# Hybrid decoder trunk on one core: the second mixer's weight rests, guards and gate products move from GpSimd to VectorE, and its convolution reads PSUM

## The chip, the cores and the metric

The kernel runs on one core of a Trainium2 chip. The metric is the device time of one execution in microseconds (us); lower is better. Engines are named as the profile names them: PE is TensorE (matmul), PEld its weight load, DVE VectorE, ACT ScalarE, POOL GpSimd, SP SyncE, which issues the DMAs.

## The reference, cut to what matters

The trunk has two layers. Each is a token mixer (layer 0: Mamba-2 SSD; layer 1: RG-LRU) and a gated convolutional MLP, each with an RMSNorm before and after it. The change is in the second mixer:

```python
LRU_WIDTH = 1280; LRU_HEADS = 10; LRU_CONV = 4; LRU_C = 8.0; SEQ = 512; D_MODEL = 1024

def causal_dwconv(x, w, b):
    k = w.shape[0]
    s = x.shape[1]
    xp = jnp.pad(x, ((0, 0), (k - 1, 0), (0, 0)))
    y = b
    for j in range(k):
        y = y + xp[:, j:j + s, :] * w[j]
    return y

def rglru_mixer(u, w_in, b_in, conv_w, conv_b, w_gx, b_gx, w_ga, b_ga, lam, w_out, b_out):
    proj = u @ w_in + b_in
    ybr = jax.nn.gelu(proj[..., :LRU_WIDTH])
    xbr = causal_dwconv(proj[..., LRU_WIDTH:], conv_w, conv_b)
    xh = xbr.reshape(bsz, s, LRU_HEADS, LRU_BLOCK)
    gx = jax.nn.sigmoid(einsum('bshi,hij->bshj', xh, w_gx) + b_gx)
    ga = jax.nn.sigmoid(einsum('bshi,hij->bshj', xh, w_ga) + b_ga)
    log_a = LRU_C * ga * jax.nn.log_sigmoid(lam)
    a_t = jnp.exp(log_a)
    mult = jnp.sqrt(-jnp.expm1(2.0 * log_a))
    b_t = mult * gx * xbr
    _, h = lax.associative_scan(_linear_combine, (a_t, b_t), axis=1)
    return (h * ybr) @ w_out + b_out
```

All inputs are float32. The convolution sees zeros ahead of the first token, and the input bias b_in is part of what it sees from the first token on.

## The kernel before, in words

Everything lies transposed: 128 channels on the partitions, the 512 tokens along the free dimension. Each float32 product is three fp32r matmuls. A weight tile is split by `Weight` (lines 199 to 214) into a high part (an ACT copy, line 209) and a low part, the rest (a subtraction, line 210, on DVE unless the argument `lo` names another engine). `Act` (line 234) splits an activation in the same way (lines 240 and 241). `up_mm` (lines 223 to 229) is one 128-channel tile of a projection: 24 matmuls of 512 tokens. A raw weight lies in one of four buffers `r` until its rest has been taken, so the next load of that buffer waits for the rest.

The second mixer is `lru` (line 556). It has three stages.

1. Ten channel tiles m of the recurrent branch. For each: the projection into a PSUM bank; an ACT copy to SBUF that adds the input bias (line 578), after which the bank is free; the convolution of four taps (`conv`, line 297: one ACT instruction for tap 3 and the bias, then three DVE instructions, line 300, for the other taps); the split of the result; six gate matmuls (lines 585 to 587); two sigmoids on ACT (lines 593 and 594); the product of one gate with the branch (line 597, DVE); a guard, max(gate, 0), on POOL (line 598); a Tanh on ACT (line 599). The projections have four PSUM banks, the gates four.
2. Once the last Tanh is done, ten exponentials (line 606, ACT, after a table load), five instructions each of lines 608 and 609 (DVE), 610 and 613 (ACT) and 615 (DVE) on 1024 columns, and ten scans (line 617, DVE).
3. Ten projections of the gating branch, which need the weights alone and are run by PE among the stages above; their GELUs (line 625) follow the last square root; the product of scan and GELU (line 628) is on POOL. Then `down` (line 254) multiplies by `w_out`: 24 matmuls (line 251) for each of ten tiles.

In the mixer the rests of the 16 projection tiles that `lru` loads itself and of its three gate weights are taken on POOL (`lo=G`). The constants (taps, biases, the rate lambda) are laid out once by `late_consts` (line 696) during the first mixer.

Program order on each engine is not written by hand: the Tile framework schedules the instructions by its own timing model, and each engine then runs its list in order, waiting on semaphores. So an instruction whose operand is late holds up all that stand behind it on its engine.

Of the kernel before, what the change touches and what calls it, by code (L numbers as in the profile page):

```python
# [10 lines left out]
AF = mybir.ActivationFunctionType  # L11
ALU = mybir.AluOpType

P = 128
# [7 lines left out]
LW = 1280  # L22
NL = LW // P
# [52 lines left out]
def tile_trunk(ctx: ExitStack, tc: tile.TileContext, x, norm_mix_pre, norm_mix_post, norm_ffn_pre, norm_ffn_post,  # L76
               ssd_w_in, ssd_conv_w, ssd_conv_b, ssd_dt_bias, ssd_a_log, ssd_d, ssd_norm, ssd_w_out,
               lru_w_in, lru_b_in, lru_conv_w, lru_conv_b, lru_w_gx, lru_b_gx, lru_w_ga, lru_b_ga,
               lru_lambda, lru_w_out, lru_b_out, ffn_w_up, ffn_conv_w, ffn_conv_b, ffn_w_down, out, layers=4):
# [3 lines left out]
    V, A, G, T = nc.vector, nc.scalar, nc.gpsimd, nc.tensor  # L83
# [7 lines left out]
    small_tiles = {n: cp.tile([r, w], F32, name=n) for n, r, w in (  # L91
        ("ident", P, P), ("nhalf", P, 4), ("ones", P, 1), ("mask", P, P), ("dch", P, NH // 2), ("hb32", NH, 4), ("hrow", 2, NH), ("dall", P, NH),
        ("cssd", P, 120), ("clru", P, 116), ("cffn0a", P, 128), ("cffn0b", P, 128), ("cffn1a", P, 128), ("cffn1b", P, 128),
        ("lam0", P, NL), ("lam1", P, NL), ("lam2", P, NL), ("lam3", P, NL), ("lam4", P, NL), ("pad", P, 16))}
    stats = cp.tile([P, 48, 4], F32, name="stats")

    def new_h(ph):
        return [cp.tile([P, 2, KD, 256], F32R, tag=n, name=f"{n}{ph}") for n in ("hh", "hl")]


    h = new_h(0)
    LO = Slots(cp, "w", 1024, range(NOP))
    LO.place()
    RAW, H4, S2 = Slots(cp, "r", 1024, range(NRAW)), Slots(cp, "v", 1024, range(N4)), Slots(cp, "t", 512, range(N2))
    PS = Slots(pp, "ps", 512, range(8))

    def row4():
        return (H4 if H4.ids else LO).get()

    def cols(h):  # L110
        return slice(h * 512, (h + 1) * 512)

    def load_gain(src):
        g = row4()
        dma(g.ap, src.rearrange("(o d) -> o d", o=1).to_broadcast([P, D]))
        return g
# [40 lines left out]
    def taps_of(a):  # L157
        return a.rearrange("j (m c) -> (j m) c", c=P)
# [61 lines left out]
    def up_w(w, c0, n=P, lo=None):  # L220
        return Weight([w[:, c0:c0 + n].rearrange("(k p) c -> p k c", p=P)], KD, KD * n, lo)
# [72 lines left out]
        return p  # L294


    def conv(dst, src, k, col):
        A.activation(dst, src, AF.Identity, bias=col(k), scale=col(k - 1))  # L298
        for s in range(1, k):
            V.scalar_tensor_tensor(out=dst[:, s:S], in0=src[:, 0:S - s], scalar=col(k - 1 - s), in1=dst[:, s:S],  # L300
                                   op0=ALU.mult, op1=ALU.add)
# [254 lines left out]
    def lru(h, prep, epilogue):  # L556
        w_in, w_out = lru_w_in[0], lru_w_out[0]
        M, X = PS.take(4), PS.take(4)
        clru, spl, spl2 = (consts[n] for n in ("clru", "spl", "spl2"))
        bt, th, at = ([row4() for _ in range(NL // 2)] for _ in range(3))  # L560
        wg = None
        first = ahead_of.pop(2)
        pts = [M.get() for m in range(4)]
        for tok in HALVES:
            for m in range(4):
                up_mm(pts[m], first[m], h, tok)
        for m in range(NL):
# [12 lines left out]
            conv(xb.ap, ub.ap, 4, lambda q: clru[:, 10 * q + m:10 * q + m + 1])  # L580
            xa = Act(xb.ap, LO)
            pg = [X.get(), X.get()]
            for i in range(2):
                b = 2 * (m % 4) + i
                T.matmul(pg[i].ap, wg.wh[:, b, :], xa.ah, start=True, stop=False)
                T.matmul(pg[i].ap, wg.wh[:, b, :], xa.al, start=False, stop=False)
                T.matmul(pg[i].ap, wg.wl[:, b, :], xa.ah, start=False, stop=True)
            if m % 4 == 3:
                wg.free()


            bm, thm, am = (s[m // 2].ap[:, cols(m % 2)] for s in (bt, th, at))
            A.activation(bm, pg[0].ap, AF.Sigmoid, bias=clru[:, 70 + m:71 + m])
            A.activation(am, pg[1].ap, AF.Sigmoid, bias=clru[:, 80 + m:81 + m])
            for s in pg:
                s.free()
            V.tensor_tensor(out=bm, in0=bm, in1=xb.ap, op=ALU.mult)
            G.tensor_scalar(out=am, in0=am, scalar1=0.0, scalar2=None, op0=ALU.max)
            last = A.activation(thm, am, AF.Tanh, scale=spl[:, m:m + 1])
            for s in (ub, xb, xa):  # L600
                s.free()
        ahead = [up_w(w_in, m * P, lo=G) for m in range(4)]
        with tc.issue_after(last.ins):
            for m in range(NL):
                am = at[m // 2].ap[:, cols(m % 2)]
                last = A.activation(am, am, AF.Exp, scale=spl2[:, m:m + 1])
        for j in range(NL // 2):
            V.scalar_tensor_tensor(out=bt[j].ap, in0=at[j].ap, scalar=1.0, in1=bt[j].ap, op0=ALU.add, op1=ALU.mult)
            V.scalar_tensor_tensor(out=at[j].ap, in0=at[j].ap, scalar=1.0, in1=th[j].ap, op0=ALU.add, op1=ALU.mult)
            A.activation(at[j].ap, at[j].ap, AF.Identity, bias=ones[:, 0:1])  # L610
        with tc.issue_after(last.ins):
            for j in range(NL // 2):
                last = A.activation(th[j].ap, th[j].ap, AF.Sqrt, scale=-1.0)
        for j in range(NL // 2):
            V.tensor_tensor(out=bt[j].ap, in0=bt[j].ap, in1=th[j].ap, op=ALU.mult)
            for i in range(2):
                V.tensor_tensor_scan(th[j].ap[:, cols(i)], at[j].ap[:, cols(i)], bt[j].ap[:, cols(i)], 0.0, op0=ALU.mult, op1=ALU.add)  # L617
        M.give(X)
        for m in range(NL):
            w, pt = ahead.pop(0) if ahead else up_w(w_in, m * P, lo=G), M.get()  # L620
            up_mm(pt, w, h, FULL)
            w.free()
            yb = S2.get()
            with tc.issue_after(last.ins):
                A.activation(yb.ap, pt.ap, AF.Gelu_apprx_tanh, bias=clru[:, 50 + m:51 + m])
            pt.free()
            hm = th[m // 2].ap[:, cols(m % 2)]
            G.tensor_tensor(out=hm, in0=hm, in1=yb.ap, op=ALU.mult)
            yb.free()
        for s in at + bt + [wg]:  # L630
            s.free()
        PS.give(M)
        bo = load_gain(lru_b_out[0])

        def biased(t, acc):
            mb = row4()
            for i in range(2):
                V.tensor_tensor(out=mb.ap[:, cols(i)], in0=acc[i].ap, in1=bo.ap[:, cols(i)], op=ALU.add)
                acc[i].free()
            epilogue(t, [mb])  # L640
            if t == NT - 1:
                bo.free()

        down(w_out, NL, lambda k: th[k // 2].ap[:, cols(k % 2)], lambda k: th[k // 2].free() if k % 2 else None, prep, biased, GT)
# [49 lines left out]
    consts = {}  # L694

    def late_consts(banks):
        clru = const_cols("clru", [taps_of(lru_conv_w[0]), rows_of(lru_conv_b[0]), rows_of(lru_b_in[0]), rows_of(lru_b_gx[0]),
                                   rows_of(lru_b_ga[0]), rows_of(lru_lambda[0]), rows_of(ssd_norm[0])], banks)
        consts["clru"] = clru

        lam = [small_tiles[f"lam{i}"] for i in range(5)]
        V.tensor_scalar(out=lam[0], in0=clru[:, 90:100], scalar1=-1.0, scalar2=None, op0=ALU.mult)
        spl = softplus(*lam[1:], lam[0])
        V.tensor_scalar(out=lam[0], in0=spl, scalar1=-8.0, scalar2=None, op0=ALU.mult)
        V.tensor_scalar(out=spl, in0=spl, scalar1=-4.0, scalar2=None, op0=ALU.mult)
# [24 lines left out]
    for ph in range(layers):  # L730
# [31 lines left out]
        h = nh  # L762
# [30 lines left out]
```

## Time and profile before

| what | value |
|---|---|
| median of 3 runs | 1713.21 us (1713.0 to 1713.45) |
| profiled execution, its own time | 1712.34 us |
| span of the profiled execution | 1710.6 us, 19926 instructions |
| PE busy | 1640.6 us (96%) |
| DVE busy | 920.0 us (54%) |
| ACT busy | 713.3 us (42%) |
| POOL busy | 291.9 us (17%) |
| granted PE clock over the span | 0.984 of full speed |

The span runs from the first to the last instruction; 1.7 us of the execution's own time lie around it. Busy shares are means over stages that have different limits, so the second mixer has to be read by itself: its first matmul starts at about 951 us and its output product is done at about 1153 us. The granted clock is the share of full TensorE speed that a stretch of the trace shows.

### The profile page before, as it was taken

To read this page: it belongs to the slowest core of one execution; us is meant where nothing else is said; L and a number is where in the kernel's file an instruction comes from. 1 tells how busy PE (TensorE), PEld (TensorE's weight loads), DVE (VectorE), ACT (ScalarE), POOL (GpSimd) and SP (SyncE) were. 2 spreads that over 40 slices of the span, in tenths; PEclk is the share of its full clock that TensorE was granted. 3 is DMA by queue.
4 is the path that set the end of the run, shared out by engine and by line. 5 is a ranking of instruction groups with operands and counts; after the bars stand their busy time and mean duration, and the time that the engine had idled before them with its cause. 6 is when DMAs were issued, how large, how long until landed. Compare 5 with 4: busy or idle time off the path is not lost.

```text
span 1710.6 us, 19926 instructions
## 1 busy us (share of the span) xinstructions
PE 1640.6 (96%) x7905; PEld 1361.9 (80%) x7905; DVE 920.0 (54%) x1122; ACT 713.3 (42%) x1072; POOL 291.9 (17%) x238
## 2 busy tenths in 40 slices
PE   7979999998999999999999999697999999999998
PEld 6858888787888888888888977586888888888886
DVE  6878886646544444443343575946644444443432
ACT  5385655435333333333332576534433333333331
POOL 1012121205111111110001466513111111110000
PEclk9989999999999999999999999898999999999999
DMA  7443432234332233332333123333422333223321
GB/s 202 114 117 101 119 94 83 87 101 135 110 88 85 87 86 87 86 96 92 109 111 111 32 82 103 109 113 87 124 85 80 95 86 87 86 75 103 115 78 50
DMA packets 235701, 166.25 MB, mean 97 GB/s; under 512 B 6604, under 2 KB 218808, under 8 KB 235608
## 3 DMA queue, kind: packets, MB, share of 16 engines
q1 hardware_dynamic: 235608, 164.98, 33.0%
q8 instruction: 62, 1.02, 0.2%
q14 instruction: 31, 0.25, 0.0%
HBM read 162.80 MB, written 2.16 MB: 96 GB/s over the span
## 4 chain that ended last, share of the span: by engine, by line
PE 84%; DVE 6%; ACT 3%; DMA 2%; POOL 2%; issue 2%; SPq 0%; DVEq 0%; POOLq 0%; ACTq 0%
PE ps L251 23%; PE ps L228 17%; PE ps L227 17%; PE ps L229 17%; PE ps L553 5%; DVE t L300 1%; PE ps L430 1%; DVE w L617 1%; DVE w L210 1%; ACT w L209 1%; PE ps L432 1%; PE ps L179 1%; DVE w L241 1%; PE ps L444 1%; DMA r<-in_ffn_w_up_dram 1%
## 5 line engine op out<-in xcount | busy, mean ns | idle before, releaser
L228 PE MATMUL ps<-hl,w 128*128 128x512 f32 (+2 forms) x1632 | 615.7, 378 | 5.8 <-DVE hl L183 5.8
L210 DVE TENSOR_TENSOR w<-r,w 128x1024 fp32r<-128x1024 f32 (+1 forms) x263 | 327.8, 1252 | 542.6 <-ACT w L209 338.5
L227 PE MATMUL ps<-hh,w 128*128 128x512 f32 (+2 forms) x1632 | 614.3, 378 | 5.2 <-ACT hh L182 2.2
L229 PE MATMUL ps<-hh,w 128*128 128x512 f32 (+2 forms) x1632 | 613.7, 377 | 0.0
L209 ACT ACTIVATE w<-r 128x1024 fp32r<-128x1024 f32 (+1 forms) x282 | 294.2, 1051 | 395.6 <-PE ps L228 137.4
L251 PE MATMUL ps<-w,w 128*128 128x512 f32 x1776 | 407.0, 391 | 13.0 <-DVE w L241 13.0
L251 PEld LDWEIGHTS ps<-w,w 128*128 128x128 f32 x1776 | 334.9, 189 | 82.9 <-DVE w L241 13.4
L228 PEld LDWEIGHTS ps<-hl,w 128*128 128x128 f32 (+1 forms) x1632 | 310.0, 190 | 61.6 <-DVE hl L183 6.7
L227 PEld LDWEIGHTS ps<-hh,w 128*128 128x128 f32 (+1 forms) x1632 | 309.5, 190 | 62.2 <-ACT hh L182 3.3
L229 PEld LDWEIGHTS ps<-hh,w 128*128 128x128 f32 (+1 forms) x1632 | 309.8, 190 | 53.8
L681 POOL TENSOR_TENSOR w<-t,t 128x512 f32<-128x512 f32 x48 | 61.6, 1284 | 461.7 <-DVE t L300 443.6
L300 DVE SCALAR_TENSOR_TENSOR t<-ps,cffn0a,t 128x511 f32<-128x511 f32 (+1 forms) x128 | 95.5, 746 | 18.7 <-ACT t L298 16.5
L300 DVE SCALAR_TENSOR_TENSOR t<-ps,cffn1a,t 128x511 f32<-128x511 f32 (+1 forms) x128 | 95.3, 746 | 15.9 <-ACT t L298 13.8
L553 PE MATMUL ps<-w,w 128*128 128x512 f32 x384 | 90.0, 392 | 3.5 <-DVE w L241 1.2
L162 POOL TENSOR_SCALAR stats<-stats 128x1 f32<-128x1 f32 x32 | 14.6, 457 | 442.8 <-ACT v L190 369.6
L298 ACT ACTIVATE t<-ps,cffn0b 128x512 f32<-128x512 f32 x64 | 49.3, 770 | 92.4 <-PE ps L229 92.4
L553 PEld LDWEIGHTS ps<-w,w 128*128 128x128 f32 x384 | 71.4, 188 | 19.9 <-DVE w L241 2.3
L298 ACT ACTIVATE t<-ps,cffn1b 128x512 f32<-128x512 f32 x64 | 49.3, 771 | 89.1 <-PE ps L229 89.1
L676 ACT ACTIVATE t<-t 128x512 f32<-128x512 f32 x64 | 40.5, 632 | 93.8 <-DVE t L300 93.8
L240 ACT ACTIVATE w<-w 128x512 fp32r<-128x512 f32 (+1 forms) x62 | 40.0, 648 | 53.6 <-PE ps L251 36.8
L210 POOL TENSOR_TENSOR w<-r,w 128x1024 fp32r<-128x1024 f32 (+1 forms) x19 | 49.4, 2609 | 32.2 <-ACT w L209 28.0
L300 DVE SCALAR_TENSOR_TENSOR t<-ps,cssd,t 128x509 f32<-128x509 f32 (+2 forms) x72 | 51.9, 736 | 3.6 <-ACT t L298 3.2
(174 smaller groups left out, 1068.1 us busy)
## 6 DMA issues: line engine op xcount, KB each, us to landing
r<-in_ffn_w_up_dram SPq DMA_DIRECT2D x128, 512.0 KB, 4.0
r<-in_ffn_w_down_dram SPq DMA_DIRECT2D x64, 512.0 KB, 3.6
r<-in_ssd_w_in_dram SPq DMA_DIRECT2D x40, 512.0 KB, 3.9
r<-in_lru_w_in_dram SPq DMA_DIRECT2D x20, 512.0 KB, 3.7
w<-cs_d SPq DMA_DIRECT2D x16, 512.0 KB, 5.2
r<-in_ssd_w_out_dram SPq DMA_DIRECT2D x16, 512.0 KB, 3.8
r<-in_lru_w_out_dram SPq DMA_DIRECT2D x10, 512.0 KB
xr<-in_x_dram SPq DMA_DIRECT2D x8, 256.0 KB, 4.3
```

Source lines behind the costliest of these rows:

```text
L209: A.activation(self.hi.ap[:, 0:n], r, AF.Copy)
L210: (lo or V).tensor_tensor(out=self.lo.ap[:, 0:n], in0=r, in1=self.hi.f[:, 0:n], op=ALU.subtract)
L227: T.matmul(o, w.wh[:, k, :], hh[:, :, k, :], start=(k == 0), stop=False)
L228: T.matmul(o, w.wh[:, k, :], hl[:, :, k, :], start=False, stop=False)
L229: T.matmul(o, w.wl[:, k, :], hh[:, :, k, :], start=False, stop=(k == KD - 1))
L240: A.activation(self.ah, ap, AF.Copy)
L251: T.matmul(acc[h].ap, x_[:, tk], w_[:, cols(h)], start=(first and i == 0), stop=(last and i == 2))
L298: A.activation(dst, src, AF.Identity, bias=col(k), scale=col(k - 1))
L300: V.scalar_tensor_tensor(out=dst[:, s:S], in0=src[:, 0:S - s], scalar=col(k - 1 - s), in1=dst[:, s:S], op0=ALU.mult, op1=ALU.add)
L553: T.matmul(acc.ap, a[:, tk], b[:, u, :], start=(j == 0 and u == 0 and i == 0), stop=(j == 7 and u == 1 and i == 2))
L676: A.activation(ga.ap, ga.ap, AF.Gelu_apprx_tanh)
L681: G.tensor_tensor(out=p[-1].ap[:, cols(m % 2)], in0=ga.ap, in1=va.ap, op=ALU.mult)
```

## The change

What it does, all in or for `lru`:

- the rests of the weights (line 210) that `lru` loads, 16 projection tiles and three gate weights, are taken on DVE; the guard (line 598) and the product with the GELU (line 628) are DVE instructions too;
- the ACT copy with the input bias (line 578) is gone. The convolution reads the projection in PSUM. The input bias times the sum of the taps is added to the convolution's own bias; the first three columns, which see fewer taps, are corrected by a DVE addition of 128x3 elements for each tile;
- `late_consts` works out that bias and the three corrections in a new constant `lcor` (11 DVE instructions of 128x10); the buffer takes the place of an unused one (`pad`).

```diff
@@ conv
-    def conv(dst, src, k, col):
-        A.activation(dst, src, AF.Identity, bias=col(k), scale=col(k - 1))
+    def conv(dst, src, k, col, bias=None):
+        A.activation(dst, src, AF.Identity, bias=col(k) if bias is None else bias, scale=col(k - 1))
         for s in range(1, k):
             V.scalar_tensor_tensor(out=dst[:, s:S], in0=src[:, 0:S - s], scalar=col(k - 1 - s), in1=dst[:, s:S],
                                    op0=ALU.mult, op1=ALU.add)
@@ lru
-                wg = Weight([w_[0, m:m + n].rearrange("h i o -> i h o") for w_ in (lru_w_gx, lru_w_ga)], n, n * 256, G)
+                wg = Weight([w_[0, m:m + n].rearrange("h i o -> i h o") for w_ in (lru_w_gx, lru_w_ga)], n, n * 256)
...
-                w, pt = up_w(w_in, LW + m * P, lo=G), M.get()
+                w, pt = up_w(w_in, LW + m * P), M.get()
                 up_mm(pt, w, h, FULL)
             w.free()
-            ub, xb = S2.get(), S2.get()
-            A.activation(ub.ap, pt.ap, AF.Identity, bias=clru[:, 60 + m:61 + m])
+
+            xb = S2.get()
+            conv(xb.ap, pt.ap, 4, lambda q: clru[:, 10 * q + m:10 * q + m + 1], lcor[:, m, 3:4])
             pt.free()
-            conv(xb.ap, ub.ap, 4, lambda q: clru[:, 10 * q + m:10 * q + m + 1])
+            V.tensor_tensor(out=xb.ap[:, 0:3], in0=xb.ap[:, 0:3], in1=lcor[:, m, 0:3], op=ALU.add)
             xa = Act(xb.ap, LO)
...
             V.tensor_tensor(out=bm, in0=bm, in1=xb.ap, op=ALU.mult)
-            G.tensor_scalar(out=am, in0=am, scalar1=0.0, scalar2=None, op0=ALU.max)
+            V.tensor_scalar(out=am, in0=am, scalar1=0.0, scalar2=None, op0=ALU.max)
             last = A.activation(thm, am, AF.Tanh, scale=spl[:, m:m + 1])
...
-        ahead = [up_w(w_in, m * P, lo=G) for m in range(4)]
+        ahead = [up_w(w_in, m * P) for m in range(4)]
...
-            w, pt = ahead.pop(0) if ahead else up_w(w_in, m * P, lo=G), M.get()
+            w, pt = ahead.pop(0) if ahead else up_w(w_in, m * P), M.get()
...
-            G.tensor_tensor(out=hm, in0=hm, in1=yb.ap, op=ALU.mult)
+            V.tensor_tensor(out=hm, in0=hm, in1=yb.ap, op=ALU.mult)
@@ late_consts
+        lcor = small_tiles["lcor"].rearrange("p (m j) -> p m j", j=4)
+        b, part = clru[:, 60:70], lam[2]
+        for q in range(4):
+            V.tensor_tensor(out=part if q else lam[3], in0=clru[:, 10 * q:10 * q + 10], in1=b, op=ALU.mult)
+            if q:
+                V.tensor_tensor(out=lam[3], in0=lam[3], in1=part, op=ALU.add)
+            if q < 3:
+                V.tensor_scalar(out=lcor[:, :, 2 - q], in0=lam[3], scalar1=-1.0, scalar2=None, op0=ALU.mult)
+        V.tensor_tensor(out=lcor[:, :, 3], in0=lam[3], in1=clru[:, 40:50], op=ALU.add)
+        consts["lcor"] = lcor
```

In the changed kernel the lines of `lru` from the product on stand one higher: 598 is the product, 599 the guard, 609 to 618 the second stage, 629 the product with the GELU; 581 is the correction. The scheduler writes the order anew. Three places of it, first on POOL, from the last guards of the first stage on. Before:

```order
L210 TENSOR_TENSOR w_1132_7789<-r_1130_7786,w_1131_7788 128x1024
L210 TENSOR_TENSOR w_1138_7801<-r_1136_7798,w_1137_7800 128x1024
L598 TENSOR_SCALAR w_1038_7145<-w_1038_7145 128x512
L210 TENSOR_TENSOR w_1135_7795<-r_1133_7792,w_1134_7794 128x1024
L598 TENSOR_SCALAR w_1039_7146<-w_1039_7146 128x512 x2
L210 TENSOR_TENSOR w_1154_7998<-r_1152_7995,w_1153_7997 128x1024
```

The guards of the last three tiles (w_1038, w_1039) stand behind weight rests. All 39 such rows leave POOL: between the norms of the layer's start and those of its end nothing is left on it. The second place is DVE at the end of the first stage and the start of the second. Before:

```order
L597 TENSOR_TENSOR v_1028_7135<-v_1028_7135,t_1102_7643 128x512
L597 TENSOR_TENSOR w_1029_7136<-w_1029_7136,t_1114_7704 128x512
L597 TENSOR_TENSOR w_1029_7136<-w_1029_7136,t_1123_7758 128x512
L608 SCALAR_TENSOR_TENSOR v_1025_7132<-w_1035_7142,v_1025_7132 128x1024
L608 SCALAR_TENSOR_TENSOR v_1026_7133<-w_1036_7143,v_1026_7133 128x1024
```

Now:

```order
L210 TENSOR_TENSOR w_1125_7796<-r_1123_7793,w_1124_7795 128x1024
L598 TENSOR_TENSOR w_1029_7147<-w_1029_7147,t_1105_7706 128x512
L241 TENSOR_TENSOR w_1114_7765<-t_1113_7759,w_1114_7765 128x512
L599 TENSOR_SCALAR w_1039_7157<-w_1039_7157 128x512
L210 TENSOR_TENSOR w_1149_8033<-r_1147_8030,w_1148_8032 128x1024
L598 TENSOR_TENSOR w_1029_7147<-w_1029_7147,t_1113_7759 128x512
L599 TENSOR_SCALAR w_1039_7157<-w_1039_7157 128x512
L210 TENSOR_TENSOR w_1144_7999<-r_1142_7996,w_1143_7998 128x1024
L609 SCALAR_TENSOR_TENSOR v_1025_7143<-w_1035_7153,v_1025_7143 128x1024
L210 TENSOR_TENSOR w_1154_8067<-r_1152_8064,w_1153_8066 128x1024
```

The last guard (L599) stands right behind the last product (L598), and rests (L210) stand between the steps. The third place is DVE from the last scans to the split of the first tile for the output product (L241, w_1179). Now:

```order
L616 TENSOR_TENSOR w_1029_7147<-w_1029_7147,w_1034_7152 128x1024
L629 TENSOR_TENSOR w_1030_7148<-w_1030_7148,t_1130_7875 128x512
L629 TENSOR_TENSOR w_1030_7148<-w_1030_7148,t_1132_7903 128x512
L618 SCALAR_TENSOR_TENSOR w_1032_7150<-w_1037_7155,v_1027_7145 128x512 x2
L618 SCALAR_TENSOR_TENSOR w_1033_7151<-w_1038_7156,v_1028_7146 128x512 x2
L210 TENSOR_TENSOR w_1182_8212<-r_1180_8209,w_1181_8211 128x1024
L629 TENSOR_TENSOR w_1031_7149<-w_1031_7149,t_1134_7931 128x512
L629 TENSOR_TENSOR w_1031_7149<-w_1031_7149,t_1136_7959 128x512
L618 SCALAR_TENSOR_TENSOR w_1034_7152<-w_1039_7157,w_1029_7147 128x512 x2
L241 TENSOR_TENSOR w_1179_8182<-w_1030_7148,w_1179_8182 128x512
```

Four products with the GELU (L629) and one rest now stand among the scans (listed as L618 SCALAR_TENSOR_TENSOR), ahead of that split; before, two rests of `w_out` stood there and no product.

## Rows read from the trace of the kernel before

**Rows 1.** PE's waits, 950 to 1110 us: who waited for whom, us in total, times, longest.

```profile
PE ps L251 <- DVE w L241: 13.0, 1, 13.0
PE ps L586 <- DVE w L241: 3.5, 3, 1.4
PE ps L585 <- ACT v L593: 2.3, 2, 1.4
```

**Rows 2.** Stretches of the second mixer: us, busy us (xcount) by engine, clock, DMA.

```profile
1060.00:1077.00 17.00, 17.00 (x76) 13.86 (x74) 17.00 (x12) 15.18 (x16) 6.44 (x2) 1.00 0.31 91
1077.00:1104.00 27.00, 12.39 (x54) 9.87 (x54) 27.00 (x17) 12.48 (x19) 18.49 (x9) 0.84 0.27 87
1104.00:1111.00 7.00, 7.00 (x20) 5.49 (x21) 6.17 (x8) 3.23 (x4) 2.88 (x1) 0.63 0.69 206
```

**Rows 3.** PE timeline: start us, us, engine line op out<-in xcount [idle before <-releaser].

```profile
977.28 0.40 PE L227 MATMUL ps<-hh,w 128*128 128x512 f32 x1
...
1103.81 8.49 PE L251 MATMUL ps<-w,w 128*128 128x512 f32 x25 [12.98 <-DVE w L241]
```

**Rows 4.** ACT timeline around the last sigmoid and the exponentials' table load.

```profile
1039.86 0.70 ACT L594 ACTIVATE w<-ps,clru 128x512 f32<-128x512 f32 x1
1044.17 1.06 ACT L209 ACTIVATE w<-r 128x1024 fp32r<-128x1024 f32 x1 [3.62 <-DMA r<-in_lru_w_in_dram]
...
1051.89 0.71 ACT L599 ACTIVATE w<-w,lam 128x512 f32<-128x512 f32 x1
1052.62 1.28 ACT L606 ACT_TABLE_LOAD   x1
```

**Rows 5.** POOL timeline: the last guards, and a rest in the second stage.

```profile
1046.22 2.94 POOL L598 TENSOR_SCALAR w<-w 128x512 f32<-128x512 f32 x2
...
1065.63 3.25 POOL L210 TENSOR_TENSOR w<-r,w 128x1024 fp32r<-128x1024 f32 x1 [1.24 <-ACT w L209]
```

**Rows 6.** DVE timeline from the second stage's start to the output product.

```profile
1055.29 4.57 DVE L608 SCALAR_TENSOR_TENSOR v<-w,v 128x1024 f32<-128x1024 f32 x2 [12.76 <-ACT w L606]
...
1066.53 3.43 DVE L609 SCALAR_TENSOR_TENSOR w<-w,w 128x1024 f32<-128x1024 f32 x1
1069.88 1.21 DVE L608 SCALAR_TENSOR_TENSOR w<-w,w 128x1024 f32<-128x1024 f32 x1
1071.02 1.21 DVE L609 SCALAR_TENSOR_TENSOR w<-w,w 128x1024 f32<-128x1024 f32 x1
...
1075.56 2.33 DVE L617 TENSOR_TENSOR_SCAN w<-w,v 128x512 f32<-128x512 f32 x2
1077.81 1.19 DVE L210 TENSOR_TENSOR w<-r,w 128x1024 fp32r<-128x1024 f32 x1
...
1095.52 4.36 DVE L617 TENSOR_TENSOR_SCAN w<-w,w 128x512 f32<-128x512 f32 x2
```

**Rows 7.** DVE's waits, 966 to 1104 us.

```profile
DVE t L300 <- ACT t L298: 14.0, 4, 6.3
...
DVE v L597 <- ACT v L593: 2.9, 2, 2.8
...
DVE w L241 <- ACT w L240: 2.8, 3, 1.3
DVE w L597 <- ACT w L593: 2.6, 2, 2.3
```

**Rows 8.** The convolution's line by tile: xcount: ns min/median/max, first and last start us.

```profile
L300 DVE SCALAR_TENSOR_TENSOR t<-ps,cffn1a,t x128: 735/748/753, 1199.9 to 1531.3; 128x511 f32<-128x511 f32 x64, 128x510 f32<-128x510 f32 x64
...
L300 DVE SCALAR_TENSOR_TENSOR t<-t,clru,t x30: 731/748/2892, 973.0 to 1033.7; 128x511 f32<-128x511 f32 x10, 128x510 f32<-128x510 f32 x10, 128x509 f32<-128x509 f32 x10
```

**Rows 9.** Prices by group, whole program: busy us, mean ns of one | idle before.

```profile
L241 DVE TENSOR_TENSOR w<-w,w 128x512 fp32r<-128x512 f32 x58 | 39.4, 684 | 6.2 <-ACT w L240 6.2
...
L284 DVE TENSOR_SCALAR t<-t 32x512 f32<-32x512 f32 x1 | 0.4, 407 | 0.0
L284 DVE TENSOR_SCALAR lam<-lam 128x10 f32<-128x10 f32 x1 | 0.2, 166 | 0.0
```

More of the change, by code (lines that the diff above doesn't have):

```diff
@@ L93, in tile_trunk @@
         ("cssd", P, 120), ("clru", P, 116), ("cffn0a", P, 128), ("cffn0b", P, 128), ("cffn1a", P, 128), ("cffn1b", P, 128),
-        ("lam0", P, NL), ("lam1", P, NL), ("lam2", P, NL), ("lam3", P, NL), ("lam4", P, NL), ("pad", P, 16))}
+        ("lam0", P, NL), ("lam1", P, NL), ("lam2", P, NL), ("lam3", P, NL), ("lam4", P, NL), ("lcor", P, 4 * NL))}
     stats = cp.tile([P, 48, 4], F32, name="stats")
@@ L558, in lru @@
         M, X = PS.take(4), PS.take(4)
-        clru, spl, spl2 = (consts[n] for n in ("clru", "spl", "spl2"))
+        clru, spl, spl2, lcor = (consts[n] for n in ("clru", "spl", "spl2", "lcor"))
         bt, th, at = ([row4() for _ in range(NL // 2)] for _ in range(3))
@@ L597, in lru @@
             V.tensor_tensor(out=bm, in0=bm, in1=xb.ap, op=ALU.mult)
-            G.tensor_scalar(out=am, in0=am, scalar1=0.0, scalar2=None, op0=ALU.max)
+            V.tensor_scalar(out=am, in0=am, scalar1=0.0, scalar2=None, op0=ALU.max)
             last = A.activation(thm, am, AF.Tanh, scale=spl[:, m:m + 1])
-            for s in (ub, xb, xa):
+            for s in (xb, xa):
                 s.free()
-        ahead = [up_w(w_in, m * P, lo=G) for m in range(4)]
+        ahead = [up_w(w_in, m * P) for m in range(4)]
         with tc.issue_after(last.ins):
```

## The prediction, as it stood before the changed kernel was timed

> **What bounds the kernel now.** I read PE's waits first, since PE is busy for 96% of the span and only its waits can be won. In the second mixer PE waits 13.0 us once, for the split that feeds the output product, and 3.5 and 2.3 us in the gates [rows 1]. That one wait is the largest in the stage. The stretches show who is late: from 1060 to 1077 us PE and DVE are both busy all the time, from 1077 to 1104 DVE is busy 27.0 of 27.0 us and PE 12.4 [rows 2]. [...] So the output product, which starts at 1103.81 us [rows 3], hangs on a chain of DVE work, and the reader should follow that chain backwards.
>
> It has two legs. The first goes from the end of the last sigmoid, 1039.86 + 0.70 = 1040.56 us, to the table load of the exponentials at 1052.62 us: 12.1 us [rows 4]. Between them there is nothing but a guard and a Tanh of 0.71 us, yet the last two guards start at 1046.22 us on POOL, behind weight rests in its queue, and the last Tanh at 1051.89 us [rows 4, 5]. DVE is idle for 12.76 us meanwhile [rows 6]. The second leg is DVE from 1055.29 us to 1103.81 us, 48.5 us [rows 3, 6]. In it instructions of one shape take two durations: line 609 takes 1.21 us at 1071.02 and 3.43 us at 1066.53, when POOL runs a rest from 1065.63 for 3.25 us; two scans take 2.33 us at 1075.56 and 4.36 us at 1095.52 [rows 5, 6]. The convolution shows the same, a median of 748 ns and a maximum of 2892 [rows 8]. DVE loses that time beside POOL, and all of this POOL work leaves.
>
> **First leg.** The guard becomes a DVE instruction of 512 columns with a scalar. No such row exists; bounds are 0.41 us, the same kind on 32 partitions, and 0.68 us, a two-input instruction of 512 columns [rows 9]. I take 0.41, the same kind. In the new order an ACT split of 1.06 us stands between the last sigmoid and the last Tanh [rows 4]; the guard lies beside it. So 1.06 + 0.71 = 1.8 us in place of 12.1: **-10.3 us**. The Tanh no longer waits for POOL's queue; what it can wait for instead is the load ahead of that ACT split (below).
>
> **Second leg.** From the first instruction of the new line 609 to the split for the output product the new order has 15 instructions of 1024 columns, ten scans, five weight rests, four products with the GELU and the split. Issue to issue a 1024-column instruction takes 1071.02 - 1069.88 = 1.14 us and a scan (1077.81 - 1075.56) / 2 = 1.13 us when POOL is quiet; a rest takes 1.19 us [rows 6], a 512-column instruction with two inputs 0.68 [rows 9]. That is 17.1 + 11.3 + 6.0 + 5 x 0.68 = 37.8 us in place of 48.5: **-10.7 us**, although rests and products are added. The later six products lie beside PE's 24 matmuls for each output tile, 24 x 17.0 / 76 = 5.4 us [rows 2], and cost nothing; without that cover they are 6 x 0.68 = 4.1 us.
>
> **Will the first stage end later?** DVE gains 30 taps read from PSUM at 0.75 (the same as now, see below), ten corrections at 0.17, nine guards at 0.41, 13 full rests at 1.19 and a half one at 0.68 before the last product, beside ten splits and ten products at 0.68 [rows 6, 8, 9]: 22.5 + 1.7 + 3.7 + 15.5 + 0.7 + 13.6 = 57.7 us. It starts at 973.0 [rows 8], so DVE could be done at 1030.7. Its waits of today, 14.0 + 2.9 + 2.8 + 2.6 less the 6.3 before the start, are 16.0 us [rows 7]. With all of them it ends at 1046.7, 6 us late; rows overlap by some 6% (1.21 against 1.14), which gives back 3. The ACT copy of about 0.7 us for each tile goes, and the rests free the raw buffers sooner. I take no change of the last sigmoid; bounds are -3 and +6.
>
> **Convolution from PSUM.** The row of the last MLP reads PSUM with the same instruction: 748 ns median, against 748 from SBUF [rows 8]. So the 30 taps cost nothing more. [...] A bank is now held until the third tap has run; four banks serve the projections, so this bites only if DVE is about four tiles late.
>
> **Clock.** If the wait shrinks, the 7 us at 0.63 become full speed: 7.0 x 0.37 = **-2.6 us** [rows 2]. Bound: 0, if a wait that is left brings the low clock back.
>
> **What is new.** Rests on DVE wait for loads, and what stands behind them on DVE waits too. Today such a wait sits on ACT: 3.62 us once for the load of a projection [rows 4]. I take **+2 us**, between none and 3.6. The first gate rest, amid the norms of the layer's start, is 1.19 us more on DVE, but POOL, which works out the norms' factors, loses it: 0, bounds -1.2 and +1.2. The 11 constant instructions are 11 x 0.17 = 1.9 us of DVE in the first mixer [rows 9], beside PE's matmuls; I take 0, with 1.9 either way, since the scheduler also reorders a few instructions there and in the second MLP.
>
> **Sum.** -10.3 - 10.7 - 2.6 + 2 = -21.6 us. The output product would start near 1103.8 - 21.0 + 2 = 1084.8. Can PE be there? From 977.28 us it has six projections, ten gate sets, ten more projections and the four matmuls ahead of the split: 16 x 24 + 60 + 4 = 448, at 17.0 / 76 = 0.224 us [rows 2, 3], so 1077.6 at the earliest. DVE stays the later of the two, with a wait of some 7 us left of the 13.0. The profiled execution took 1712.34 us; less 21.6 it is 1690.7. The median of the runs is 0.9 us above it, so I forecast **1691.6 us**. A measurement of this kernel tells about 0.2%, 3.4 us, from no change.
>
> **Rivals.**
> 1. *PE becomes the bound.* The gates also come sooner and PE never waits: the product starts at 1077.6, so 26.2 + 2.6 = 28.8 us are won, 1684.4 us. For it: DVE's 57.7 us of work leave room before 1040. Against it: the second leg's 37.8 us are in series with table load and exponentials. It is the low end of the range.
> 2. *DVE's queue becomes the bound in the first stage.* The order stays interleaved, but 6 us of late end remain (less 3 of overlap) and three rests, with what is behind them, wait 3.62 us for their loads: +3 + 10.9 on top of -23.6 gives -9.7, 1703.5 us; 1697 to 1709 by how many wait. For it: three engines hand each tile to and fro, and today's list holds 16.0 us of such waits. Against it: the rests free raw buffers sooner, so loads start sooner.
> 3. *No tile overlaps the next, and it is slower.* Then each tile goes alone through three ACT steps of the convolution, split and Tanh (2.1), three taps (2.25), correction (0.17), split (0.68), six matmuls (1.34), two sigmoids (1.40), product and guard (1.09) and a rest (1.19): 10.2 us. Ten from 973.0 end at 1075.0 in place of 1040.6, +34.4 - 23.6 = +10.8, 1724.0 us. The place is DVE's list in the first stage. It decides above (1040.6 - 973.0 + 23.6) / 10 = 9.1 us for each tile; today it is 6.8. Against it: the order has up to three tiles' taps interleaved.
> 4. *The gain is used up*: a first stage some 20 to 27 us later, at about 9.1 us for each tile, 1713.
>
> **How the numbers follow.** The forecast, 1686 to 1697, has 0.62: its legs are plain sums of undisturbed rows. Rival 1 beyond it, below 1686: 0.06. Rival 2: 0.19. Rival 4: 0.06. Rival 3: 0.07. Faster by over 0.2%: 0.62 + 0.06 + 0.19 = 0.87; same 0.06; slower 0.07. The range from 1685 to 1704 takes the forecast, the edge of rival 1 and two thirds of rival 2, 0.62 + 0.04 + 0.13 = 0.79.
>
> **What would show it.** Right: PE's wait on line 241 well below 13 us; no maximum of line 300, 609 or 618 above twice its median; the table load about 2 us after the last sigmoid; some 38 us from the first line 609 to the split; no clock of 0.63 behind it. Wrong: waits of DVE on loads or on ACT above 16 us in the first stage, the last sigmoid later than 1046 us, or PE waiting for a projection's bank (a wait on line 300).

## The result, and the profile after

The changed kernel takes 1686.89 us (median of 4 runs, 1684.68 to 1687.1) against 1713.11 us for the kernel before on the same chip (4 runs, 1712.23 to 1713.45). The ratio is 0.9845 with the interval 0.983 to 0.9861, so 26.2 us are gone. The profiled execution took 1684.68 us (span 1683.0), 27.7 less than the one shown of before; it is the fastest of the four, 2.2 us below their median.

**Who waits now.** PE's waits from 950 to 1110 us: one line is left where [rows 1] begin with 13.0 us.

```profile
PE ps L251 <- DVE w L241: 0.6, 1, 0.6
```

The stretches of [rows 2], with the same columns, now read:

```profile
1060.00:1077.00 17.00, 17.00 (x76) 14.08 (x76) 17.00 (x18) 11.15 (x16) 0.00 (x0) 1.00 0.46 158
1077.00:1104.00 27.00, 26.41 (x116) 21.54 (x116) 19.84 (x26) 12.25 (x17) 0.00 (x0) 1.00 0.54 156
1104.00:1111.00 7.00, 7.00 (x32) 5.82 (x31) 4.29 (x4) 2.48 (x3) 0.00 (x0) 1.00 0.70 193
```

From 1077 to 1104 us PE is busy 26.41 of 27 us where it was busy 12.39, POOL runs nothing, and the clock of 0.63 behind the wait has become 1.00. The output product answers to [rows 3] in PE's timeline; its second group starts at 1078.26 us, 25.6 us sooner:

```profile
1076.61 1.07 PE L251 MATMUL ps<-w,w 128*128 128x512 f32 x4
1078.26 46.77 PE L251 MATMUL ps<-w,w 128*128 128x512 f32 x205 [0.58 <-DVE w L241]
```

**First leg.** ACT's timeline, beside [rows 4]:

```profile
1033.84 2.01 ACT L209 ACTIVATE w<-r 128x1024 fp32r<-128x1024 f32 x2 [4.09 <-DMA r<-in_lru_w_in_dram]
...
1036.32 0.68 ACT L595 ACTIVATE w<-ps,clru 128x512 f32<-128x512 f32 x1
1036.89 1.05 ACT L209 ACTIVATE w<-r 128x1024 fp32r<-128x1024 f32 x1
1037.84 0.71 ACT L600 ACTIVATE w<-w,lam 128x512 f32<-128x512 f32 x1
1038.57 1.28 ACT L607 ACT_TABLE_LOAD   x1
```

The last sigmoid ends at 1036.32 + 0.68 = 1037.00 us, the table load follows at 1038.57: 1.6 us in place of 12.1. Only the split stands between sigmoid and Tanh; the guard, now on DVE, lies beside it.

**Second leg.** DVE's timeline, beside [rows 5, 6]: the wait on ACT with a rest behind it, the last guard, and the leg from line 609 to the split.

```profile
1034.93 1.23 DVE L210 TENSOR_TENSOR w<-r,w 128x1024 fp32r<-128x1024 f32 x1 [5.94 <-ACT w L209]
...
1037.07 0.42 DVE L599 TENSOR_SCALAR w<-w 128x512 f32<-128x512 f32 x1
...
1041.24 1.23 DVE L609 SCALAR_TENSOR_TENSOR v<-w,v 128x1024 f32<-128x1024 f32 x1 [2.04 <-ACT w L607]
...
1053.74 2.35 DVE L610 SCALAR_TENSOR_TENSOR w<-w,w 128x1024 f32<-128x1024 f32 x2
...
1068.49 4.57 DVE L618 TENSOR_TENSOR_SCAN w<-w,v 128x512 f32<-128x512 f32 x4
...
1077.54 0.67 DVE L241 TENSOR_TENSOR w<-w,w 128x512 fp32r<-128x512 f32 x1
```

From 1041.24 to the output product at 1078.26 us it is 37.0 us in place of 48.5. No instruction is stretched: two of line 610 take 2.35 us, four scans 4.57 (two took 4.36 beside POOL).

**Waits of DVE**, 966 to 1078 us, beside [rows 7]:

```profile
DVE w L210 <- ACT w L209: 12.9, 6, 5.9
DVE t L300 <- ACT t L298: 4.9, 2, 4.8
```

The rests do wait, 12.9 us in all, for splits on ACT. The longest of these waits, 5.9 us, is for a split that itself waits 4.09 us for its load (above); the other splits of ACT wait for PE in this stage (6.4 us in all) and not for loads. The taps' waits fell from 14.0 to 4.9 us, nearly all of it the start. Line 300, beside [rows 8]:

```profile
L300 DVE SCALAR_TENSOR_TENSOR t<-ps,clru,t x30: 734/743/752, 969.4 to 1021.9; 128x511 f32<-128x511 f32 x10, 128x510 f32<-128x510 f32 x10, 128x509 f32<-128x509 f32 x10
```

The maximum of 2892 ns is gone. For the first stage one more stretch is worth a look, here of the kernel before:

```profile
977.00:1040.00 63.00, 57.15 (x240) 44.52 (x239) 46.76 (x47) 41.94 (x63) 37.32 (x18) 0.98 0.27 79
```

and of the changed one:

```profile
977.00:1040.00 63.00, 63.00 (x280) 52.18 (x279) 47.15 (x75) 42.60 (x62) 0.00 (x0) 1.00 0.38 109
```

DVE runs 28 instructions more (75 against 47) in the same busy time, 47.15 against 46.76 us; POOL's 37.32 us are gone; and PE is busy all the time.

### The profile page after: what moved, and what is told of

It is laid out like the page before. It is cut to its first block, busy times and chain, and to the rows that moved or that the text cites. A ratio compares the mean times of both kernels' runs of the same rounds, so it can differ in the third digit from the quotient of the medians.

```text
span 1683.0 us, 19923 instructions
## 1 busy us (share of the span) xinstructions
PE 1633.1 (97%) x7905; PEld 1358.6 (81%) x7905; DVE 917.7 (55%) x1182; ACT 706.1 (42%) x1062; POOL 204.4 (12%) x199
## 5 line engine op out<-in xcount | busy, mean ns | idle before, releaser
L210 DVE TENSOR_TENSOR w<-r,w 128x1024 fp32r<-128x1024 f32 (+1 forms) x282 | 349.3, 1245 | 552.0 <-ACT w L209 351.4
L300 DVE SCALAR_TENSOR_TENSOR t<-ps,cssd,t 128x511 f32<-128x511 f32 (+2 forms) x72 | 52.1, 736 | 3.4 <-ACT t L298 3.0
L419 ACT ACTIVATE w<-w,t 128x128 f32<-128x128 f32 x128 | 39.1, 389 | 30.3 <-DMA w<-cs_d 20.8
```

Of the source, the lines that this page charges most:

```text
L210: (lo or V).tensor_tensor(out=self.lo.ap[:, 0:n], in0=r, in1=self.hi.f[:, 0:n], op=ALU.subtract)
```

## The experiments

The change has four parts: rests, guards and products moved to DVE, and the convolution. First each was made alone in the kernel before, then each was undone in the changed one. Ratios are to the kernel before, run on the same chip.

**Guards alone.**

```diff
-            G.tensor_scalar(out=am, in0=am, scalar1=0.0, scalar2=None, op0=ALU.max)
+            V.tensor_scalar(out=am, in0=am, scalar1=0.0, scalar2=None, op0=ALU.max)
```

> The kernel before, with the guard (line 598) alone moved to DVE. Theory: the first leg, last sigmoid to table load, was the guard standing behind weight rests in POOL's queue, so it falls from 12.1 us to 2 or 3, the second leg stays near 48 us, and the time falls by about 9 us to 1704 (1701 to 1707). Rival (the queue is not the cause, the tiles are late anyway): within 2 us of 1713.

Measured: 1716.13 us, ratio 1.0015 (1.0006 to 1.0025). A miss. PE's waits, 950 to 1120 us:

```profile
PE ps L251 <- ACT t L625: 11.1, 2, 6.1
PE ps L251 <- DVE w L241: 5.7, 1, 5.7
```

Neither leg does what was expected of it. ACT's last sigmoid and the table load:

```profile
1044.54 0.68 ACT L594 ACTIVATE w<-ps,clru 128x512 f32<-128x512 f32 x1
...
1050.46 1.28 ACT L606 ACT_TABLE_LOAD   x1
```

The first leg is 5.2 us and not 2 or 3, and the last sigmoid ends at 1045.22 us, 4.7 later than before: ahead of it on ACT stands a Tanh that waits 4.06 us for its guard on DVE. So the table load comes only 2.2 us sooner. The output product comes 10.9 us sooner all the same, its matmuls go on at 1092.94 us instead of 1103.81; the other 8.7 us are in the second leg, 39.8 us in place of 48.5, in which DVE's new list has the split for the output product ahead of the last two scans and two rests, and the first two instructions of line 608 undisturbed (2.45 us in place of 4.57). But PE gains nothing by it: in the new list it starts the output product before the last GELUs have emptied their PSUM banks, and on ACT each of these GELUs stands behind the split of a `w_out` tile that waits for its load. ACT's timeline:

```profile
1101.01 1.06 ACT L209 ACTIVATE w<-r 128x1024 fp32r<-128x1024 f32 x1 [6.46 <-DMA r<-in_lru_w_out_dram]
1101.97 0.67 ACT L625 ACTIVATE t<-ps,clru 128x512 f32<-128x512 f32 x1
...
1109.82 2.00 ACT L209 ACTIVATE w<-r 128x1024 fp32r<-128x1024 f32 x2 [6.66 <-DMA r<-in_lru_w_out_dram]
1111.72 0.67 ACT L625 ACTIVATE t<-ps,clru 128x512 f32<-128x512 f32 x1
```

PE goes on at 1112.45 us, when the GELU of 1111.72 is done. So 13.0 us of wait became 16.8. A guard on DVE is also not cheap while POOL still runs rests. DVE's timeline:

```profile
1041.94 0.41 DVE L598 TENSOR_SCALAR w<-w 128x512 f32<-128x512 f32 x1
...
1047.07 2.61 DVE L598 TENSOR_SCALAR w<-w 128x512 f32<-128x512 f32 x1
```

and POOL's:

```profile
1044.19 7.75 POOL L210 TENSOR_TENSOR w<-r,w 128x1024 fp32r<-128x1024 f32 x3 [2.72 <-ACT w L209]
```

**Rests alone.**

```diff
-                wg = Weight([w_[0, m:m + n].rearrange("h i o -> i h o") for w_ in (lru_w_gx, lru_w_ga)], n, n * 256, G)
+                wg = Weight([w_[0, m:m + n].rearrange("h i o -> i h o") for w_ in (lru_w_gx, lru_w_ga)], n, n * 256)
...
-                w, pt = up_w(w_in, LW + m * P, lo=G), M.get()
+                w, pt = up_w(w_in, LW + m * P), M.get()
...
-        ahead = [up_w(w_in, m * P, lo=G) for m in range(4)]
+        ahead = [up_w(w_in, m * P) for m in range(4)]
...
-            w, pt = ahead.pop(0) if ahead else up_w(w_in, m * P, lo=G), M.get()
+            w, pt = ahead.pop(0) if ahead else up_w(w_in, m * P), M.get()
```

> The kernel before, with the weight rests alone moved to DVE; guards and products stay on POOL. Theory: guards find POOL empty, first leg about 3 us; in the second leg lines 608 and 609 run undisturbed (-6.6 us) but share DVE with some five rests (+6), and scans still stretch beside the products; together -9 us, 1704 (1700 to 1707). Rival (POOL does not disturb DVE, and 22 us more on DVE is what counts): 1713 or slower.

Measured: 1693.2 us, ratio 0.9881 (0.9866 to 0.9896), 21.3 us less: more than twice what was expected. The rests are in both legs: the table load comes at 1040.14 us although the guards are still on POOL (first leg 2.3 us), and the second leg, 37.6 us, loses its 3.4 us instructions of line 609. What is left is the products on POOL beside the scans. POOL's timeline, then DVE's:

```profile
1063.97 17.52 POOL L628 TENSOR_TENSOR w<-w,t 128x512 f32<-128x512 f32 x8 [24.61 <-ACT t L625]
```

```profile
1058.80 2.33 DVE L617 TENSOR_TENSOR_SCAN w<-w,v 128x512 f32<-128x512 f32 x2
...
1069.92 8.81 DVE L617 TENSOR_TENSOR_SCAN w<-w,v 128x512 f32<-128x512 f32 x4
```

Four scans take 2.2 us each there, two before it 1.2.

**Products alone.**

```diff
-            G.tensor_tensor(out=hm, in0=hm, in1=yb.ap, op=ALU.mult)
+            V.tensor_tensor(out=hm, in0=hm, in1=yb.ap, op=ALU.mult)
```

> The kernel before, with the products with the GELU (line 628) alone moved to DVE. Theory: first leg unchanged at 12 us; in the second leg the scans and line 615 are no longer stretched (ten scans 17.0 to about 11.5 us, five of line 615 9.2 to 5.7) against four products more on DVE (2.5): -6.8 us, 1706 (1703 to 1709). Rival (products are off the path): within 2 us of 1713, or slower by the 2.5 us.

Measured: 1706.67 us, ratio 0.9957 (0.9942 to 0.9972). The first leg is as before (the table load at 1053.38 us); the second leg is 43.3 us, and PE's wait for the split falls to 4.3 us.

**Convolution alone**, with the change's lines in `conv` and `late_consts`, and in `lru`:

```diff
-            ub, xb = S2.get(), S2.get()
-            A.activation(ub.ap, pt.ap, AF.Identity, bias=clru[:, 60 + m:61 + m])
+            xb = S2.get()
+            conv(xb.ap, pt.ap, 4, lambda q: clru[:, 10 * q + m:10 * q + m + 1], lcor[:, m, 3:4])
             pt.free()
-            conv(xb.ap, ub.ap, 4, lambda q: clru[:, 10 * q + m:10 * q + m + 1])
+            V.tensor_tensor(out=xb.ap[:, 0:3], in0=xb.ap[:, 0:3], in1=lcor[:, m, 0:3], op=ALU.add)
```

> The kernel before, with the convolution alone changed: it reads PSUM, the copy is gone, the bias is folded; rests, guards and products stay on POOL. Theory: the taps have one SBUF input in place of two and no longer stretch beside POOL's rests (maximum under 0.9 us against 2.89), but both legs stay as they are, 12 and 48 us, so 1709 (1705 to 1713). Rival (the copy and the bank it frees are where the gain is): 1700 or less.

Measured: 1710.14 us, ratio 0.9975 (0.9964 to 0.9986). The tap's line, with 19 weight rests of `lru` still on POOL:

```profile
L300 DVE SCALAR_TENSOR_TENSOR t<-ps,clru,t x30: 734/748/753, 973.3 to 1031.3; 128x511 f32<-128x511 f32 x10, 128x510 f32<-128x510 f32 x10, 128x509 f32<-128x509 f32 x10
```

No tap is stretched here: with one input in PSUM the slowest of the 30 takes 753 ns, against 2892 from SBUF [rows 8]. Around one long stretch of rests on POOL one sees both kinds on DVE:

```profile
1028.43 7.57 POOL L210 TENSOR_TENSOR w<-r,w 128x1024 fp32r<-128x1024 f32 x3
```

```profile
1027.69 1.53 DVE L300 SCALAR_TENSOR_TENSOR t<-ps,clru,t 128x511 f32<-128x511 f32 x2 [3.36 <-ACT t L298]
1029.14 2.25 DVE L598 TENSOR_TENSOR w<-w,t 128x512 f32<-128x512 f32 x1
1031.31 0.73 DVE L300 SCALAR_TENSOR_TENSOR t<-ps,clru,t 128x509 f32<-128x509 f32 x1
```

The legs do not stay as they are: the first is 4.1 us (1039.26 to 1043.36) although guards and rests are both still on POOL, and the second 40.9, again with the split ahead of the last two scans. The gain is small for the reason seen with the guards: the output product goes on at 1086.91 us, 16.9 sooner, but PE then waits 9.8 us for GELUs.

**Each part undone in the changed kernel.** The guards go back to POOL:

```diff
-            V.tensor_scalar(out=am, in0=am, scalar1=0.0, scalar2=None, op0=ALU.max)
+            G.tensor_scalar(out=am, in0=am, scalar1=0.0, scalar2=None, op0=ALU.max)
```

> The changed kernel with the guard back on POOL, where nothing else is left in that stage. Theory: it was the queue, not the engine: the guard takes some 1.5 us in place of 0.42, first leg 1.6 to about 2.8 us, 1688 (1686 to 1690). Rival (POOL as such delays the last Tanh): 1695 or more.

The products go back:

```diff
-            V.tensor_tensor(out=hm, in0=hm, in1=yb.ap, op=ALU.mult)
+            G.tensor_tensor(out=hm, in0=hm, in1=yb.ap, op=ALU.mult)
```

> The changed kernel with the products with the GELU back on POOL. Theory: scans and line 616 stretch again beside them (up to +9.2 us) and four products leave DVE (-2.5): +6 us, PE waits about 6 us for line 241, 1693 (1690 to 1697). Rival (PE is the bound, DVE has room): 1687 to 1688.

The rests go back, at all four calls as in this one:

```diff
-        ahead = [up_w(w_in, m * P) for m in range(4)]
+        ahead = [up_w(w_in, m * P, lo=G) for m in range(4)]
```

> The changed kernel with the weight rests back on POOL; guards and products stay on DVE. Theory: DVE loses 22 us of work but its instructions with two SBUF inputs stretch again wherever a rest runs beside them; the second leg stays near 37 us (-6 for the rests, +6.6 for lines 609 and 610), the first at 2 us, the gates come a little later: 1690 (1687 to 1695). Rival (DVE's work is what counts): 1684 to 1686.

The convolution reads the copy in SBUF again:

```diff
-            conv(xb.ap, pt.ap, 4, lambda q: clru[:, 10 * q + m:10 * q + m + 1], lcor[:, m, 3:4])
+            A.activation(ub.ap, pt.ap, AF.Identity, bias=clru[:, 60 + m:61 + m])
...
+            conv(xb.ap, ub.ap, 4, lambda q: clru[:, 10 * q + m:10 * q + m + 1])
```

> The changed kernel with the convolution as before (ACT copy with the bias, taps from SBUF). Theory: with POOL empty the taps take 0.75 us from SBUF as well; ten copies of 0.69 us go back to ACT, which has room; 1687 (1686 to 1690). Rival (the bank freed later or the copy decides): over 1692, or under 1685.

| kernel | us | ratio, interval |
|---|---|---|
| the change | 1686.89 | 0.9845 (0.983 to 0.9861) |
| guards undone | 1688.21 | 0.9847 (0.9832 to 0.9862) |
| products undone | 1696.2 | 0.9895 (0.9879 to 0.9912) |
| rests undone | 1694.09 | 0.988 (0.9866 to 0.9895) |
| convolution undone | 1686.18 | 0.9838 (0.9823 to 0.9852) |

With the products undone DVE's scans are slow again beside POOL. DVE's timeline, then POOL's:

```profile
1071.42 8.81 DVE L618 TENSOR_TENSOR_SCAN w<-w,v 128x512 f32<-128x512 f32 x4
```

```profile
1064.43 18.56 POOL L629 TENSOR_TENSOR w<-w,t 128x512 f32<-128x512 f32 x8 [103.46 <-ACT t L626]
```

With the rests undone two steps of the second leg are, again with DVE first:

```profile
1051.31 3.42 DVE L609 SCALAR_TENSOR_TENSOR v<-w,v 128x1024 f32<-128x1024 f32 x1
...
1056.92 3.43 DVE L610 SCALAR_TENSOR_TENSOR w<-w,w 128x1024 f32<-128x1024 f32 x1
```

```profile
1050.37 3.27 POOL L210 TENSOR_TENSOR w<-r,w 128x1024 fp32r<-128x1024 f32 x1 [4.60 <-ACT w L209]
1056.65 2.61 POOL L210 TENSOR_TENSOR w<-r,w 128x1024 fp32r<-128x1024 f32 x1 [3.02 <-ACT w L209]
```

PE's waits alone do not make up these times. With the products undone PE waits 4.6 us from 950 to 1120 us (2.1 for the split, where about 6 were expected, and 2.5 for a GELU), with the rests undone 3.1 for the split. The granted clock is lower too, 0.95 in both kernels from 1040 to 1110 us. That stretch, with the columns of [rows 2], first with the products undone, then with the rests undone:

```profile
1040.00:1110.00 70.00, 65.33 (x273) 53.09 (x272) 59.04 (x49) 44.27 (x57) 25.29 (x10) 0.95 0.43 134
```

```profile
1040.00:1110.00 70.00, 66.89 (x283) 54.79 (x282) 58.53 (x56) 45.09 (x57) 11.50 (x5) 0.95 0.46 135
```

With the change the clock is 1.00 there. 70 us at 0.95 cost an estimated 3.5 us, so waits and clock, less the 0.6 us of wait of the change, come to 7.5 and 6.0 us; by the ratios the two kernels lose 8.6 and 6.0.

Products and rests carry the gain; with them in place guards and convolution cannot be told from nothing. The first leg with the guards undone is 3.4 us: the guards are POOL's only work in the stage there, 19.75 us for the ten (2.0 each), and the last Tanh waits 0.77 us for its guard. The parts do not add up: alone they give +1.7, -21.3, -7.8 and -4.3 us, -31.8 in all against 26.2 measured, since guards, rests and convolution shorten the same first leg, and PE takes over. With the convolution undone PE shows no wait at all from 950 to 1120 us, and the time is the same.

**The guards left out.** This kernel leaves out max(gate, 0), ten DVE instructions.

> The changed kernel without the guard: max(gate, 0) is left out. Theory: in the changed kernel PE is the bound of the stage, so 4 us less on DVE change the time by less than 1 us: 1686 to 1687. Rival (DVE's chain still sets the end): 2 to 4 us faster, 1683 to 1685.

Measured: 1687.28 us, ratio 0.9843 (0.9828 to 0.9857). DVE work of 10 x 0.42 us taken from the first stage changes nothing: DVE is no longer the bound.

**POOL beside DVE, by itself.** DVE's work stays that of the change; POOL gets ten instructions back that nobody needs, each after a scan on what the scan has read. In one kernel it reads and writes:

```diff
                 V.tensor_tensor_scan(th[j].ap[:, cols(i)], at[j].ap[:, cols(i)], bt[j].ap[:, cols(i)], 0.0, op0=ALU.mult, op1=ALU.add)
+                G.tensor_tensor(out=bt[j].ap[:, cols(i)], in0=bt[j].ap[:, cols(i)], in1=bt[j].ap[:, cols(i)], op=ALU.mult)
```

and in the other it only writes:

```diff
+                G.memset(bt[j].ap[:, cols(i)], 0.0)
```

> The changed kernel with ten products of 128x512 elements added on POOL, each on the half of a buffer that a scan has just used up; DVE's list is the same. Theory: POOL instructions that read two SBUF inputs stretch scans and line 616 from 1.2 to some 2.2 us, as in the kernel before: second leg 37 to about 46 us, PE waits about 9 us, 1696 (1692 to 1700). Rival (the stretching came from semaphores or the buffers shared with the products): within 2 us of 1687.

> As the run with ten products added on POOL, but each is a memset of the same 128x512 elements, which reads nothing. If POOL's reads are what DVE waits for: no stretching, 1687. If any POOL access to SBUF is: as with the products, scaled by the shorter time of a memset, 1690 to 1696. I expect the first.

Measured: 1697.41 us, ratio 0.9903 (0.9888 to 0.9918), with reads; 1686.96 us, ratio 0.9839 (0.9824 to 0.9853), with writes alone. Lines 618 and 619 with reads (ns minimum, median, maximum):

```profile
L618 DVE TENSOR_TENSOR_SCAN w<-w,v x8: 1193/1211/1994, 1059.8 to 1077.5; 128x512 f32<-128x512 f32 x8
L619 POOL TENSOR_TENSOR v<-v x8: 1804/1954/2017, 1061.2 to 1080.3; 128x512 f32<-128x512 f32 x8
```

and with writes alone:

```profile
L618 DVE TENSOR_TENSOR_SCAN w<-w,v x8: 1202/1210/1227, 1061.1 to 1074.7; 128x512 f32<-128x512 f32 x8
L619 POOL MEMSET v<- x8: 526/526/529, 1062.5 to 1076.0; 128x512 f32 x8
```

Beside POOL's reads a scan takes up to 1.99 us in place of 1.21, and PE's wait for the split grows from 0.6 to 9.0 us; beside its writes that wait is 0.5 us. DVE's list is not quite the same with reads: one product more stands ahead of the split, 0.6 us undisturbed. Otherwise this is direct: nobody reads what POOL writes there, so no wait for a result is in it. The writes are also shorter (0.53 against 1.95 us), so less of DVE's time lies beside them; but none of the eight scans is longer than 1227 ns.

**One step further.** The same move for the residual addition (line 194), which only the last norm had on DVE:

```diff
-(V if final else G).tensor_tensor(out=xr
+V.tensor_tensor(out=xr
```

> The changed kernel with the addition to the residual at the ends of the first three sub-layers (line 194, POOL, two of 1.28 us for each 128 tokens) on DVE too. Theory: this addition stands on the chain that PE waits for there (line 172, 19.8 us of waits in all); 2 x 0.6 us less for each of three ends' last tokens and some at the others': 1683 (1680 to 1686). Rival (the chain has another path, or DVE is late there): 1686 to 1688.

Measured: 1679.09 us (1678.68 to 1680.68), ratio 0.9797 (0.9781 to 0.9814): faster than both kernels, and more than expected. The groups of line 194 in the changed kernel, and what ACT's next instruction (line 169) waits for:

```profile
L169 ACT ACTIVATE v<-xr 128x512 f32<-128x512 f32 x24 | 15.1, 630 | 24.5 <-POOL xr L194 20.0 <-DMA xr<-in_x_dram 4.5
L194 POOL TENSOR_TENSOR xr<-xr,v 128x512 f32<-128x512 f32 x16 | 22.4, 1420 | 6.2 <-DVE v L193 6.2
L194 POOL TENSOR_TENSOR xr<-xr,w 128x512 f32<-128x512 f32 x8 | 13.9, 1760 | 3.5 <-DVE w L193 3.5
```

and in this one:

```profile
L194 DVE TENSOR_TENSOR xr<-xr,v 128x512 f32<-128x512 f32 x24 | 15.5, 683 | 0.0
L169 ACT ACTIVATE v<-xr 128x512 f32<-128x512 f32 x24 | 15.0, 626 | 21.9 <-DVE xr L194 16.8 <-DMA xr<-in_x_dram 5.1
```

An addition of 1.42 or 1.76 us becomes one of 0.68 in a chain for which PE waits. Of the 24 additions 16 lie ahead of the second mixer, from 395.8 us on, so the gain is not one of this stage alone: over the whole program PE's waits on line 172 fall from 12.0 and 7.8 to 10.4 and 6.4 us. That is 3.0 of the 5.5 us between the two profiled executions; the rest is not traced to one wait.

## Why the prediction was right, point by point

The time, 1686.89 us, lies in the forecast's own stretch of 1686 to 1697, at its fast end: 26.2 us were won where 21.6 were forecast. The two legs are as forecast. What is left behind them is not: PE is the bound, as rival 1 has it, and that the median lies on the forecast's side of 1686 is in part luck, for the profiled execution, 1684.68 us, lies on the rival's.

- **First leg**: forecast 1.8 us, measured 1.6. The guard's price of 0.41 [rows 9] held: 0.42. The reading of the 12.1 us was short of a step. In the kernel before the last guard is done at 1049.16 us, and the last Tanh still waits on ACT behind two splits, of which the first waits for a load:

```profile
1049.98 2.01 ACT L209 ACTIVATE w<-r 128x1024 fp32r<-128x1024 f32 x2 [1.52 <-DMA r<-in_lru_w_in_dram]
```

So 2.7 of the 12.1 us were ACT's and not POOL's queue. That the leg hangs on what the lists put ahead of the last guard and Tanh, and not on the guard's engine, the runs bear out: it is 3.4 us with the guards undone, and 4.1 with the convolution alone.

- **Second leg**: forecast 37.8 us, measured 37.0, as the sum of undisturbed rows. That rows of POOL beside DVE were the cause is shown by the two runs with idle POOL work: a scan takes up to 1.99 us beside POOL's products and at most 1.23 beside its memsets.
- **Clock**: forecast -2.6 us, and the clock is 1.00 in all three stretches. But the forecast took this beside a wait of 7 us that was left, and the two did not go together in the runs: with the rests undone, where 3.1 us of wait were left, the clock was 0.95 from 1040 to 1110 us. The term came right with 0.6 us of wait left.
- **Convolution from PSUM**: forecast no cost; the median tap is 743 ns against 748 from SBUF. What the forecast missed is a benefit: the taps are no longer stretched beside POOL (maximum 753 ns beside rests with the convolution alone, 2892 before). In the full change, without rests on POOL, it is worth nothing.
- **Mis-sized: "I take no change of the last sigmoid".** It ends 3.6 us sooner (1037.00 against 1040.56). That comes ahead of the stage: the first tap starts at 969.4 us instead of 973.0, and from first tap to last sigmoid it is 67.6 us in both kernels. Of the 3.6 us, 1.6 are the ACT copy that is gone ahead of the first tap: from the first read of PSUM to the first tap it is 2.37 us (970.64 to 973.01) in the kernel before and 0.81 in the kernel with the convolution alone. Another 1.35 are the gate rest that left POOL amid the norms: ACT waits 3.40 us there instead of 4.75, and 4.78 again with the rests undone. That term stood at 0, with -1.2 as its bound. Some 0.7 lie earlier still and are put down to no part of the change: executions scatter by more, as the first read of PSUM starts at 968.58 us here and at 971.52 in the run with POOL's writes, whose code is the same up to there.
- **Mis-sized: "+2 us" for the new waits on loads.** DVE's rests wait 12.9 us for splits, one of them (5.9 us) by way of a load, but none of it reached PE. The sum had DVE as the last one in the first stage (57.7 us of work and 16.0 of waits from 973.0 us on). Its busy time stayed at 47 us with 28 instructions more, because what it gained is what it had lost beside POOL; PE is busy 63.00 of 63.00 us there.
- **"DVE stays the later of the two, with a wait of some 7 us left."** 0.6 us is left. The product starts at 1078.26 us, 0.7 after the floor of 1077.6 that the text gives for PE. That it meets this floor so closely is luck in part: PE began those 448 matmuls at 975.94 us, 1.3 sooner than in the kernel before, but issues one every 0.227 us (1075.25 to 1075.93 for three) and not every 0.224. PE waits for 0.6 us alone, so rival 1's bound is the one that holds; guards left out or convolution undone make no difference any more.
- **Rivals 2, 3 and 4** needed a first stage that ends later, held up on DVE; it ends sooner.

By the rows: -10.5 (first leg), -11.5 (second) and -3.6 (last sigmoid) make the 25.6 us by which the product starts sooner, and with -2.6 for the clock 28.2; the two profiled executions are 27.7 apart.

What the text did not foresee is that parts of the change alone hand their gain to another wait. The guards' place in POOL's queue was told rightly, yet moving them alone gained nothing: the last sigmoid came 4.7 us later, the first leg kept 5.2 us, and what the second leg gave went to GELUs that the new list put behind loads. Whether an order written by hand would give the guards alone more was not tried.

## What to carry to other kernels

When one instruction shape has two durations in a trace, look at what runs beside it on POOL: here work moved from POOL to a DVE that was 100% busy in its stage made that leg 11.5 us shorter. Price such a move by the undisturbed rows, and ask next which engine takes over, here PE within a microsecond of its floor. Where a scheduler writes the lists, a part tried alone is a new order as well, so read who waits behind whom in its trace before its time is taken as that part's worth. And count with a wait of PE the clock behind it: here 3.1 us of wait came with an estimated 3.5 us of low clock.

## What the runs showed of the hardware

- Beside POOL instructions that read SBUF, DVE instructions with two SBUF inputs took longer: scans of 1.21 us took up to 1.99 beside added products on POOL (the run with reads), and four took 8.81 us beside the products with the GELU (products undone) in place of 4.57 (the change). Beside a memset on POOL (0.53 us), which reads nothing, no scan took more than 1.23 us.
- DVE instructions with one SBUF input and one in PSUM did not: the taps took at most 753 ns with rests on POOL (the convolution alone), against 2892 with both inputs in SBUF (the kernel before).
- The guard has only one SBUF input and yet took 2.61 us beside a rest on POOL and 0.41 between two stretches of rests (guards alone). Why it was held up is not shown.
- PE's granted clock was lower with a short wait too: 0.95 from 1040 to 1110 us with one wait of 3.1 us in it (rests undone), 1.00 with one of 0.6 (the change) or 1.1 (guards undone).
